# Mixing stage of a two-layer trunk: two weight casts a layer on GpSimd, two kinds of VectorE instruction pinned in program order, and the pooled products in another order

## The chip, the cores and the metric

The kernel runs on one core of one Trainium2 chip. The metric is the device time of one execution in microseconds. The kernel before has a median of 1299.72 us over three runs (1299.27 to 1299.83).

## The reference

A trunk of two layers works on 256 positions of 1024 channels in float32. Each layer is a feed-forward half step, a mixing stage with three branches, a second half step and an embedding added through a gate. Cut to what matters here:

```python
def layer(h):
    h = h + 0.5 * swiglu(rmsnorm(h, ffn1_norm), ffn1_w_gate, ffn1_w_up, ffn1_w_down)
    u = rmsnorm(h, mix_norm)
    (q, c_kv, q_idx, w_idx, k_idx, x_pool, z, xbc, dt_raw, gate_raw) = split(u @ w_in)
    y_attn = dsa_attention(q, rmsnorm(c_kv), q_idx, w_idx, rmsnorm(k_idx), w_uk, w_uv)
    y_pool = pool_mixer(x_pool, pool_w, pool_scale)      # windows 2, 4, 8, 16: mean less identity
    y_ssd = ssd_mixer(z, xbc, dt_raw, ...)               # Mamba-2, 2 chunks of 128
    g_attn, g_pool, g_ssd = split(sigmoid(gate_raw), 3)
    h = h + (g_attn * (y_attn @ w_br_attn) + g_pool * (y_pool @ w_br_pool)
             + g_ssd * (y_ssd @ w_br_ssd)) @ w_out
    h = h + 0.5 * swiglu(rmsnorm(h, ffn2_norm), ffn2_w_gate, ffn2_w_up, ffn2_w_down)
    return h + sigmoid(rmsnorm(h, ple_norm) @ ple_w_gate) * (p @ ple_w_proj)
# two layers, then a last rmsnorm
```

The attention chooses 64 keys for each position by an indexer's scores, and then takes a softmax over them with 8 heads. The Mamba branch multiplies by decay factors, which are exponentials of running sums of rates. The pooled branch is a running mean over a window, less the input, times a small matrix for each of four groups of 128 channels.

## The kernel before

Activations lie transposed, with channels on the partitions and the 256 positions along a row. To keep float32 accuracy on TensorE, every number is split in two parts in the format that PE multiplies here (fp32r in the rows): a high part (a cast) and a low part (the number less its high part). Each product is then three matmuls into one bank: high weight by high activation, high weight by low activation, low weight by high activation. In `mm3` these are lines 211, 212 and 213.

Weights come in units of 128 x 1024. `load` (lines 141 to 150) issues the load on the queue of SyncE (L144), the cast to the high part `whi` on ScalarE (L145) and the subtraction that gives the low part `wlo` on VectorE (L146). Four raw buffers and five each for the parts go round, and a unit is loaded up to four units ahead of its use. So a unit passes through a DMA, ScalarE and VectorE before PE can have all of it, and a cast can begin only when PE has done with the unit that had the buffer. One of the five pairs is kept for the matrix of the pooled branch during the mixing.

The mixing projects the input with 56 column tiles, one unit each. The last 24 (units `U_IN` + 32 to `U_IN` + 55) are the gates. While PE works through them, the Mamba states (`ssd`), the softmax (`softmax`, `attention`) and the pooled groups (`pool_group`) run on the other engines. They are four generators, and `weave` takes steps from them in turns by a number of steps that each is given. This stretch lies near 290 to 370 us in layer 0 and 643 us later in layer 1.

A scheduler that runs when the program is built puts the instructions of each engine in order, by durations and waits that it estimates for itself. It may move an instruction past others of its engine. Two marks hold it back: `keep_in_program_order`, which keeps the marked instructions of an engine in the order in which they are written, and the issue tokens of `turn`. Each engine then works through its list strictly in that order, and an instruction that waits holds up all behind it.

The lines that the change and the prediction speak of:

- In `softmax`, for each of two groups of scores: the maxima with the mask added (L921, VectorE, reading the scores in PSUM), the exponentials with their sums (L923, ScalarE), the reciprocal of the sums (L925, VectorE), the scaling (L927, ScalarE), and then PE's transposes (L114), copied out of PSUM in L939. The first softmax is over 128 keys, the later ones over 256.
- In `ssd`: the running sums of the rates (L1099, scans on VectorE), their exponentials (L1104, ScalarE), a copy of the last column (L1107), the product of the decay factors with a matrix `cb` (L1108, VectorE), the addition of a finished part (L1124), and a second kind of scan and exponential (L1135, L1136). GpSimd multiplies the input by the step size in L1085.
- In `pool_group`: the window sums by doubling, a copy and an add for each (L1168, L1169), a correction of the first columns (L1173), the mean less the input (L1176), its high part on ScalarE (L1181) and its low part (L1183), for one group on GpSimd and for the others on VectorE. The three products follow in L1188 by way of `mm3`.
- L256 and L260 are low parts of other activations (`split` and `split_scaled`), L259 is the high part that goes with L260.

## Time and profile before

| | |
|---|---|
| median of 3 runs | 1299.72 us |
| the profiled execution | 1300.84 us, span 1299.1 us |
| PE busy | 1290.3 us (99%), clock 1.000 |
| VectorE (DVE) busy | 1046.3 us (81%) |
| ScalarE (ACT) busy | 739.5 us (57%) |
| GpSimd (POOL) busy | 17.9 us (1%) in 27 instructions |
| casts of weight units (L145) | 456 of them, 1045 ns each |
| subtractions for the low part (L146) | 456 of them, 1215 ns each |
| the stretch 290 to 365 us (75 us) | PE 74.35, DVE 64.96, ACT 53.91, POOL 5.73 us busy |

In a row of the timeline the first number is the start in us from the span's beginning, the second the duration; then come engine, line, operation, output and inputs, shapes and count. A bracket gives the idle time of the engine just before and what ended it. An instruction's duration includes its end in the pipeline, so that the next one on the same engine can start some 0.1 us before it is over. PE and PEld are the matmuls and the weight loads that go with them. A matmul's duration (276 ns) is longer than the step from one to the next for the same reason.

### The profile page before, as it was taken

Reading aid. Unit: us, or ns where it says so; the run is one execution under the profiler, and the core shown is the slowest. Engines: PE = TensorE matmul, PEld = TensorE weight load, DVE = VectorE, ACT = ScalarE, POOL = GpSimd, SP = SyncE. Lnnn points to the kernel's source line nnn. Section 1 sums busy time; section 2 is a strip of 40 time slices with the busy share of each in tenths; the row PEclk is TensorE's granted clock in tenths of the full one; section 3 lists DMA queues with packets and bytes.
Section 4 is the critical chain, followed back from the end, with each engine's and each line's share of the span. In section 5 each row is a group of like instructions: output and inputs, shape, how many; then the busy total and the mean of one; then the engine's idle time right before and its main releaser. Section 6 shows DMA issues by size and latency. Waiting matters only on the chain.

```text
span 1299.1 us, 28286 instructions
## 1 busy us (share of the span) xinstructions
PE 1290.3 (99%) x11398; PEld 1282.0 (99%) x11398; DVE 1046.3 (81%) x1935; ACT 739.5 (57%) x1209; POOL 17.9 (1%) x27
## 2 busy tenths in 40 slices
PE   9999999999999999999999999999999999999998
PEld 9999999999999999999999999999999999999998
DVE  7877669987999887766997776799879989777667
ACT  6644446666874555544654444476667646544455
POOL 0000000000000000000000000000100000000000
PEclk9999999999999999999999999999999999999999
DMA  7766646586647576666556665556965566655661
GB/s 251 247 193 195 194 158 211 179 222 205 188 142 235 162 227 194 195 191 194 188 195 194 194 196 191 162 192 184 212 224 165 183 199 211 197 195 193 194 194 66
DMA packets 89571, 250.51 MB, mean 193 GB/s; under 512 B 25184, under 2 KB 27872, under 8 KB 89440
## 3 DMA queue, kind: packets, MB, share of 16 engines
q1 hardware_dynamic: 89008, 247.92, 60.6%
q8 instruction: 89, 1.46, 0.5%
q10 hardware_dynamic: 432, 0.79, 0.2%
q14 instruction: 42, 0.34, 0.1%
HBM read 245.50 MB, written 1.08 MB: 190 GB/s over the span
## 4 chain that ended last, share of the span: by engine, by line
PE 87%; DVE 7%; ACT 2%; DMA 2%; issue 2%; DVEq 0%; SPq 0%; ACTq 0%
PE mm L213 27%; PE mm L212 27%; PE mm L211 27%; DVE wlo L146 2%; DVE ct L1099 1%; PE aux L111 1%; ACT whi L145 1%; DMA gh<-rates 1%; DMA raw<-in_w_dram 1%; PE mm L230 1%; PE mm L227 1%; PE aux L213 1%; PE aux L212 1%; ACT t L923 1%; PE mm L225 1%
## 5 line engine op out<-in xcount | busy, mean ns | idle before, releaser
L145 ACT CAST whi<-raw 128x1024 fp32r<-128x1024 f32 (+1 forms) x456 | 475.1, 1045 | 484.9 <-PE mm L212 353.8
L146 DVE TENSOR_TENSOR wlo<-raw,whi 128x1024 fp32r<-128x1024 f32 (+1 forms) x456 | 552.2, 1215 | 170.1 <-ACT whi L145 162.2
L212 PE MATMUL mm<-ul,whi 128*128 128x256 f32 x2438 | 672.0, 276 | 0.0
L213 PE MATMUL mm<-uh,wlo 128*128 128x256 f32 x2438 | 671.8, 277 | 0.0
L211 PE MATMUL mm<-uh,whi 128*128 128x256 f32 x2402 | 662.3, 277 | 0.8 <-ACT whi L145 0.8
L212 PEld LDWEIGHTS mm<-ul,whi 128*128 128x128 f32 x2438 | 457.5, 188 | 0.1
L213 PEld LDWEIGHTS mm<-uh,wlo 128*128 128x128 f32 x2438 | 457.0, 188 | 0.2
L211 PEld LDWEIGHTS mm<-uh,whi 128*128 128x128 f32 x2402 | 449.8, 188 | 2.1 <-ACT whi L145 1.2
L213 PE MATMUL mm<-gh,wlo 128*128 128x256 f32 x704 | 194.1, 276 | 0.0
L212 PE MATMUL mm<-gl,whi 128*128 128x256 f32 x704 | 194.1, 276 | 0.0
L211 PE MATMUL mm<-gh,whi 128*128 128x256 f32 x704 | 193.7, 276 | 0.0
L213 PEld LDWEIGHTS mm<-gh,wlo 128*128 128x128 f32 x704 | 132.2, 188 | 0.0
L212 PEld LDWEIGHTS mm<-gl,whi 128*128 128x128 f32 x704 | 132.2, 188 | 0.0
L211 PEld LDWEIGHTS mm<-gh,whi 128*128 128x128 f32 x704 | 131.9, 188 | 0.0
L212 PE MATMUL mm<-a,whi 128*128 128x256 f32 x256 | 70.7, 276 | 0.0
L213 PE MATMUL mm<-a,wlo 128*128 128x256 f32 x256 | 70.7, 276 | 0.0
L211 PE MATMUL mm<-a,whi 128*128 128x256 f32 x256 | 70.7, 276 | 0.0
L213 PEld LDWEIGHTS mm<-a,wlo 128*128 128x128 f32 x256 | 48.1, 188 | 0.0
L211 PEld LDWEIGHTS mm<-a,whi 128*128 128x128 f32 x256 | 48.1, 188 | 0.0
L212 PEld LDWEIGHTS mm<-a,whi 128*128 128x128 f32 x256 | 48.1, 188 | 0.0
L498 DVE TENSOR_TENSOR t<-mm,rs_r 128x256 f32<-128x256 f32 x88 | 37.3, 424 | 13.2 <-PE mm L213 13.0
L499 DVE TENSOR_TENSOR t<-t,mm 128x256 f32<-128x256 f32 x87 | 36.5, 420 | 2.6
(300 smaller groups left out, 1271.1 us busy)
## 6 DMA issues: line engine op xcount, KB each, us to landing
raw<-in_w_dram SPq DMA_DIRECT2D x446, 512.0 KB, 4.3
gh<-rates SPq DMA_DIRECT2D x16, 256.0 KB, 4.1
raw<-in_w_dram SPq DMA_DIRECT2D x8, 352.0 KB, 3.0
ul<-a SPq DMA_DIRECT2D x32, 64.0 KB, 4.8
a<-in_x_dram SPq DMA_DIRECT2D x3, 512.0 KB, 5.3
gh<-rates SPq DMA_DIRECT2D x8, 128.0 KB, 4.5
a<-in_x_dram SPq DMA_DIRECT2D x1, 544.0 KB, 3.7
raw<-in_w_dram SPq DMA_DIRECT2D x2, 256.0 KB, 4.4
```

Of the source, the lines that this page charges most:

```text
L111: self.tc.keep_in_program_order(self.nc.tensor.matmul(*args, **kw))
L145: nc.scalar.copy(hi[:, :n], raw[:, :n])
L146: ins = nc.vector.tensor_tensor(lo[:, :n], raw[:, :n], hi[:, :n].bitcast(F), op=OP.subtract)
L211: (self.mm if keep else mm)(ps, a[0], b[0], start=start, stop=False)
L212: mm(ps, a[0], b[1], start=False, stop=False)
L213: mm(ps, a[1], b[0], start=False, stop=stop)
L225: (self.mm if keep and k == 0 else mm)(ps, w[0][:, s], u[0][:, k], start=k == 0, stop=False)
L227: mm(ps, w[0][:, s], u[1][:, k], start=False, stop=False)
L230: mm(ps, w[1][:, k * P:(k + 1) * P], u[0][:, k], start=False, stop=k == last)
L498: ins = [nc.vector.tensor_tensor(t, p1[0], r, op=OP.mult), nc.vector.tensor_tensor(g, t, p1[1], op=OP.mult)]
L499: nc.vector.tensor_tensor(g, t, p1[1], op=OP.mult)]
L923: self.last = nc.scalar.activation(pr[:, j], pr[:, j], AF.Exp, bias=x, scale=-1.0, accum_out=sums[:, j:j + 1])
```

## The change

Four edits, all in the mixing:

1. In `load`, two units of each layer, `U_IN` + 45 and `U_IN` + 54 (gate tiles 13 and 22), have their high part cast by GpSimd instead of ScalarE. In the lists below these are `whi_4329` and `whi_4869` in layer 0.
2. The reciprocal in `softmax` is kept in program order.
3. The decay product in `ssd` is kept in program order.
4. In `pool_group` the three matmuls are written out, so that the low weight by the high activation comes second and the high weight by the low activation last.

```diff
--- before.py
+++ after.py
@@ -142,7 +142,10 @@
         nc = self.nc
         raw, hi, lo = self.parts()
         nc.sync.dma_start(raw[:, :n], self.ins["w"][layer, u, :, :n])
-        nc.scalar.copy(hi[:, :n], raw[:, :n])
+        if u in (U_IN + 45, U_IN + 54):
+            nc.gpsimd.tensor_copy(hi[:, :n], raw[:, :n])
+        else:
+            nc.scalar.copy(hi[:, :n], raw[:, :n])
         ins = nc.vector.tensor_tensor(lo[:, :n], raw[:, :n], hi[:, :n].bitcast(F), op=OP.subtract)
         if keep:
             self.tc.keep_in_program_order(ins)
@@ -922,7 +925,7 @@
                                                1.0, 3.0e38, OP.add, OP.min, accum_out=x)
                 self.last = nc.scalar.activation(pr[:, j], pr[:, j], AF.Exp, bias=x, scale=-1.0,
                                                  accum_out=sums[:, j:j + 1])
-            nc.vector.reciprocal(sums, sums)
+            self.tc.keep_in_program_order(nc.vector.reciprocal(sums, sums))
             for j in range(per):
                 nc.scalar.mul(pr[:, j], pr[:, j], sums[:, j:j + 1])
             prs.append(pr)
@@ -1105,8 +1108,8 @@
                     if h == 0:
                         k = g * 8 + q * 4
                         nc.vector.tensor_copy(e0[:, k:k + 4], m[:, :, P - 1])
-                    nc.vector.tensor_tensor(m, m, cb[:, h, g, None].to_broadcast([P, 4, P]),
-                                            op=OP.mult)
+                    self.tc.keep_in_program_order(nc.vector.tensor_tensor(
+                        m, m, cb[:, h, g, None].to_broadcast([P, 4, P]), op=OP.mult))
                     yield
                 ps = self.bank("aux")
 
@@ -1185,7 +1188,8 @@
         yield
         po = self.bank()
         s = slice(g * P, (g + 1) * P)
-        self.mm3(po[:, :S], (wpl[0][:, s], wpl[1][:, s]), (yh, yl), True, True)
+        for w, v in ((0, yh), (1, yh), (0, yl)):
+            nc.tensor.matmul(po[:, :S], wpl[w][:, s], v, start=w == 0 and v is yh, stop=v is yl)
         self.split_scaled(yp[:, 0, g], yp[:, 1, g], po[:, :S], self.col(layer, "pool_scale", g))
```

From `load` on, a line of the kernel after has a number that is 3 higher than before, and 4 higher behind `pool_group`.

The edits move other instructions too, since the scheduler works out a new order. The queue of loads keeps its order, but for a load of the rates and a unit that change places once in each layer. GpSimd's list gets one cast behind the four products of L1085 and one behind the low part of the pooled group (L1183). On PE the transposes of the first softmax come eight matmuls earlier, ahead of the first use of `whi_4329`. The three places that follow are in layer 0; layer 1 has the same ones.

VectorE, from the unit `wlo_4747` to the first maxima of the last softmax (`t_692`); `t_700` and `t_701` are window sums, `t_681` is the mean less the input of the group whose low part GpSimd makes, `ct_4853` are the decay factors, and `uh_2747` is the Mamba branch's result. Before:

```order
L146 TENSOR_TENSOR wlo_4747<-raw_4745,whi_4746 128x1024
L1176 SCALAR_TENSOR_TENSOR t_681_4783<-t_675_4741,gl_2475 128x256
L146 TENSOR_TENSOR wlo_4792<-raw_4790,whi_4791 128x1024
L1124 TENSOR_TENSOR uh_2747<-uh_2747,aux_4789 128x4x128
L1099 SCALAR_TENSOR_TENSOR ct_4853<-gh_2474,after 128x512 x2
L1168 COPY t_700_4892<-gl_2475 128x1
L1169 TENSOR_TENSOR t_700_4892<-gl_2475 128x271
L921 ISA t_692_4857,mx_4858<-aux_4837,idxw_3617 128x256
```

and now:

```order
L1179 SCALAR_TENSOR_TENSOR t_681_4783<-t_675_4741,gl_2475 128x256
L149 TENSOR_TENSOR wlo_4747<-raw_4745,whi_4746 128x1024
L1171 COPY t_700_4892<-gl_2475 128x1
L1172 TENSOR_TENSOR t_700_4892<-gl_2475 128x271
L1127 TENSOR_TENSOR uh_2747<-uh_2747,aux_4789 128x4x128
L1102 SCALAR_TENSOR_TENSOR ct_4853<-gh_2474,after 128x512 x2
L149 TENSOR_TENSOR wlo_4792<-raw_4790,whi_4791 128x1024
L1171 COPY t_701_4895<-t_700_4892 128x2
L1172 TENSOR_TENSOR t_701_4895<-t_700_4892 128x270
L924 ISA t_692_4857,mx_4858<-aux_4837,idxw_3617 128x256
```

The mean `t_681` went ahead of the unit `wlo_4747`, the unit `wlo_4792` behind the scans, the window sum `t_700` ahead of the addition, and the copy and the add of the next window sum, `t_701`, came ahead of the maxima.

The same engine behind those maxima, down to the second reciprocal of the softmax (`sum_4859` and `sum_4908` belong to its two groups; `a_542_3897` holds the low parts of the attention's and the pooled branch's results). Before:

```order
L1108 TENSOR_TENSOR ct_4853<-ct_4853,gl_2475 128x512
L1168 COPY t_701_4895<-t_700_4892 128x2
L1169 TENSOR_TENSOR t_701_4895<-t_700_4892 128x270
L1108 TENSOR_TENSOR ct_4853<-ct_4853,gl_2475 128x512
L260 SCALAR_TENSOR_TENSOR a_542_3897<-mm_4886,cc_88,a_542_3897 128x256
L925 RECIPROCAL sum_4859<-sum_4859 128x2
L1168 COPY t_702_4898<-t_701_4895 128x4
L1169 TENSOR_TENSOR t_702_4898<-t_701_4895 128x268
L925 RECIPROCAL sum_4908<-sum_4908 128x2
```

and now:

```order
L1111 TENSOR_TENSOR ct_4853<-ct_4853,gl_2475 128x512
L1171 COPY t_702_4898<-t_701_4895 128x4
L1172 TENSOR_TENSOR t_702_4898<-t_701_4895 128x268
L263 SCALAR_TENSOR_TENSOR a_542_3897<-mm_4886,cc_88,a_542_3897 128x256
L928 RECIPROCAL sum_4859<-sum_4859 128x2
L1171 COPY t_703_4901<-t_702_4898 128x8
L1172 TENSOR_TENSOR t_703_4901<-t_702_4898 128x264
L1111 TENSOR_TENSOR ct_4853<-ct_4853,gl_2475 128x512
L928 RECIPROCAL sum_4908<-sum_4908 128x2
```

The second decay product stood ahead of both reciprocals and is now between them; the window sum `t_702` went ahead of the first reciprocal and `t_703` ahead of the second. PE meanwhile has the transposes of this softmax four matmuls earlier: twelve matmuls of the unit `whi_4746` are left behind the first of them, where eight were.

ScalarE, some 25 us earlier, from the copies of the first softmax's transposes (`aux_4412`, `aux_4413`) to the exponential of the decay factors; `t_646` is the exponential of the second kind (L1136), which waits for VectorE's scans of L1135. Before:

```order
L939 COPY t_627_4422<-aux_4412 128x512
L259 ACTIVATE a_542_3897<-mm_4458,cc_88 128x256
L939 COPY t_628_4425<-aux_4413 128x512
L145 CAST whi_4466<-raw_4465 128x1024
L1136 ACTIVATE t_646_4560<-t_646_4560 128x512
L145 CAST whi_4484<-raw_4483 128x1024
L690 ACTIVATE gh_2474<-mm_4427 128x512
L255 CAST a_542_3897<-aux_4533 128x4x128
L1104 ACTIVATE ct_4717<-ct_4717 128x512 x2
```

and now:

```order
L942 COPY t_627_4422<-aux_4412 128x512
L262 ACTIVATE a_542_3897<-mm_4458,cc_88 128x256
L942 COPY t_628_4425<-aux_4413 128x512
L1139 ACTIVATE t_646_4560<-t_646_4560 128x512
L148 CAST whi_4466<-raw_4465 128x1024
L148 CAST whi_4484<-raw_4483 128x1024
L693 ACTIVATE gh_2474<-mm_4427 128x512
L258 CAST a_542_3897<-aux_4533 128x4x128
L1107 ACTIVATE ct_4717<-ct_4717 128x512 x2
```

The cast of the unit `whi_4466` stood ahead of the exponential of `t_646` and now stands behind it.

## The prediction

> **What bounds the kernel now.** I read the page first, then the waits of PE, then the windows around the two places that the change touches, and last the instructions in order of time there.

> ```profile
> span 1299.1 us, 28286 instructions
> PE 1290.3 (99%) x11398; PEld 1282.0 (99%) x11398; DVE 1046.3 (81%) x1935; ACT 739.5 (57%) x1209; POOL 17.9 (1%) x27
> PE aux L114 <- ACT t L927: 0.8, 2, 0.4
> 333.10:361.10 28.00, 28.00 (x275) 27.06 (x272) 27.97 (x66) 21.95 (x50) 1.22 (x1) 1.00 0.58 178
> ```

> PE is busy for 99% of the span, and its granted clock is 1.00, so the end is set by PE's list of matmuls plus the few places where PE has to wait. Off PE nothing counts until it makes PE wait. The row of waits (us in total, times, longest) belongs to the softmax of layer 0 and its twin in layer 1. The last row is the window 333.1 to 361.1 of layer 0's mixing (columns: length, then PE, PEld, DVE, ACT, POOL, clock, DMA): VectorE is busy for 27.97 of 28.00 us there. It has no slack in that window, so whatever makes it late at the start is still late at the end.

> There are three stalls per layer that the change can touch. In layer 0:

> ```profile
> 323.92 1.03 ACT L145 CAST whi<-raw 128x1024 fp32r<-128x1024 f32 x1
> 324.35 0.28 PE L212 MATMUL mm<-ul,whi 128*128 128x256 f32 x1
> 324.46 0.28 PE L213 MATMUL mm<-uh,wlo 128*128 128x256 f32 x1
> 325.00 0.39 PE L211 MATMUL mm<-uh,whi 128*128 128x256 f32 x1 [0.27 <-ACT whi L145]
> 325.65 0.30 PE L114 MATMUL aux<-ident,t 128*128 128x128 f32 x1
> 355.14 0.19 PEld L212 LDWEIGHTS mm<-t,whi 128*128 128x128 f32 x1 [0.20 <-POOL t L1183]
> 358.11 0.51 ACT L923 ACTIVATE t<-t,mx 128x256 f32<-128x256 f32 x1
> 360.45 1.05 ACT L145 CAST whi<-raw 128x1024 fp32r<-128x1024 f32 x1
> 361.39 1.71 ACT L927 ACTIVATE t<-t,sum 128x256 f32<-128x256 f32 x4
> 361.95 0.44 PE L114 MATMUL aux<-ident,t 128*128 128x128 f32 x2 [0.38 <-ACT t L927]
> 967.28 0.28 PE L213 MATMUL mm<-uh,wlo 128*128 128x256 f32 x1
> 967.51 0.39 PE L211 MATMUL mm<-uh,whi 128*128 128x256 f32 x1
> ```

> Matmuls follow each other every 0.11 us (324.35, 324.46). **Stall A**, at 325.00: due at 324.57, so 0.43 is lost; the cast of 323.92 ends last. In layer 1 the same spot loses 0.12 (967.28 to 967.51, less 0.11). **Stall C**, at 355.14: the weight load waits 0.20 for GpSimd's low part of the pooled average; a restart costs 0.11 more (the matmul of 325.00 shows 0.39 instead of 0.28), together 0.3. **Stall B**, at 361.95: the transposes wait for the scaling L927, which stands behind the cast of 360.45. I count 0.55 lost, so PE asked at 361.40 (the bracket, 0.38, leaves out the load ahead of it). A, B and C of both layers together are 0.43 + 0.12 + 2 x (0.55 + 0.3) = 2.2 us, a few restarts more at most. That is all that the change can win: 0.17% of the time.

> **The change part by part.** *Two casts per layer leave ScalarE.* Each frees 0.94 us of its queue (360.45 to 361.39), just ahead of the scaling that PE waits for. That is the gain of B, if the scaling can use it.

> *VectorE's order around stall B.* These rows are the old order:

> ```profile
> 353.27 1.22 DVE L146 TENSOR_TENSOR wlo<-raw,whi 128x1024 fp32r<-128x1024 f32 x1
> 355.00 2.34 DVE L1099 TENSOR_TENSOR_SCAN ct<-gh,after 128x512 f32<-128x512 f32 x2
> 357.30 0.43 DVE L1169 TENSOR_TENSOR t<-gl 128x271 f32<-128x271 f32 x1
> 357.64 0.42 DVE L921 CUSTOM_DVE_ANT_0 t<-aux,idxw 128x256 f32<-128x256 f32 x1
> 359.02 0.69 DVE L1108 TENSOR_TENSOR ct<-ct,gl 128x512 f32<-128x512 f32 x1
> 359.62 0.16 DVE L1168 COPY t<-t 128x2 f32<-128x2 f32 x1
> 360.04 0.69 DVE L1108 TENSOR_TENSOR ct<-ct,gl 128x512 f32<-128x512 f32 x1
> 360.64 0.48 DVE L260 SCALAR_TENSOR_TENSOR a<-mm,cc,a 128x256 fp32r<-128x256 f32 x1
> 361.04 0.16 DVE L925 RECIPROCAL sum<-sum 128x2 f32<-128x2 f32 x1
> ```

> In the new order most of this is only permuted ahead of the four maxima (L921): split, scans and first doubling are still all in front. New in front is the second doubling, copy and add: 359.62 to 360.04, **0.42 us**. Behind the maxima come one decay product (359.02 to 359.62, 0.60), the third doubling (0.42), L260 (0.40) and only then the first reciprocal: maxima end + 1.42. The maxima take 357.64 to 359.02, 1.38.

> *A delay that arrives from upstream.* ScalarE's new order puts the cast of one unit behind the decay exponential L1136:

> ```profile
> 332.86 0.63 ACT L1136 ACTIVATE t<-t 128x512 f32<-128x512 f32 x1 [0.60 <-DVE t L1135]
> 333.12 1.22 DVE L146 TENSOR_TENSOR wlo<-raw,whi 128x1024 fp32r<-128x1024 f32 x1
> ```

> The cast used to be done before the exponential. Behind it (its 0.53 from 332.86) the cast starts at 333.39 and its split 0.94 later, at 334.33 instead of 333.12: 1.21 late. If the 0.94 that ScalarE saves at stall A brings all this forward, 0.27 late. I take **0.4**, near the lower end, since the queue between is ScalarE's own; VectorE's full window carries it to B.

> *The casts on GpSimd.* Its price is not in this trace. Rows to bound it (the first gives the shortest, median and longest of eight in ns):

> ```profile
> L1085 POOL TENSOR_TENSOR ul<-ul,dt x8: 1036/1038/1905, 289.6 to 936.6; 128x512 f32<-128x512 f32 x8
> L409 POOL TENSOR_SCALAR_AFFINE_SELECT tri<-ones 128x128 f32<-128x128 f32 x1 | 0.3, 290 | 0.0
> L405 POOL MEMSET ones<- 128x128 f32 x1 | 0.2, 204 | 0.3 <-POOLq L1476 0.3
> L1258 POOL TENSOR_SCALAR idxw<-idxw 128x256 f32<-128x256 f32 x1 | 0.9, 856 | 27.7 <-DMA idxw<-in_gn_dram 27.7
> L176 POOL MEMSET warm<- 128x1 f32 x1 | 0.1, 98 | 0.0
> ```

> By the memset (106 ns for 127 more elements) 1024 elements take 0.95 us; by the select 1.6; by the product with two inputs (1038 for 512) 2.1; by the scaling L1258 3.4. The cast has one input and no arithmetic and is nearest to the memset and the select: I take 1.1 us, ends 0.95 and 3.4. Even at 2.1 the casts are done long before PE needs them.

> *What they do to VectorE.* The trace holds a warning:

> ```profile
> 289.27 0.19 DVE L1030 SCALAR_TENSOR_TENSOR dt<-dt_y,dt_x 128x32 f32<-128x32 f32 x1
> 289.38 1.23 DVE L146 TENSOR_TENSOR wlo<-raw,whi 128x1024 fp32r<-128x1024 f32 x1
> 289.60 4.91 POOL L1085 TENSOR_TENSOR ul<-ul,dt 128x512 f32<-128x512 f32 x4 [22.69 <-DMA raw<-in_w_dram]
> 290.52 1.03 DVE L1031 SCALAR_TENSOR_TENSOR da<-dt,al 128x32 f32<-128x32 f32 x1
> 353.87 1.22 POOL L1183 TENSOR_TENSOR t<-t,t 128x256 fp32r<-128x256 f32 x1 [59.36 <-ACT t L1181]
> ```

> The first of the four GpSimd products, started under a split, takes 1.905 where the median is 1.038. And L1031, of the size of L1030's 0.19, takes 1.03 and ends with that product (291.5). GpSimd waited for the split; then VectorE's next instruction waited for GpSimd. L1183 at 353.87 also ends 0.6 after the split of 353.27 to 354.49. So an instruction of VectorE that reads two operands from SBUF and one of GpSimd exclude one another, whole instruction by whole instruction, and the one that has waited goes first. [...]

> At stall B two GpSimd instructions now meet VectorE in its full window. The subtraction L1183 moves up, because L1176 does, to the end of the previous split; the first doubling add, two SBUF operands, waits behind it: **0.4** (0.6 less the copy and what was overlapped). And the second cast, second in GpSimd's queue, waits for PE to free its buffer:

> ```profile
> 319.13 0.28 PE L111 MATMUL mm<-uh,whi 128*128 128x256 f32 x1
> 319.22 0.29 DVE L921 CUSTOM_DVE_ANT_0 t<-aux,idxw 128x128 f32<-128x128 f32 x1
> 356.87 0.28 PE L111 MATMUL mm<-uh,whi 128*128 128x256 f32 x1
> ```

> At 356.87 PE goes on to its next unit, which frees the buffer; after the change that is at 356.6 to 356.9. VectorE is then at the end of the scans, and next is a split of 1.2 us, then the maxima. The cast gets in, and the split waits for it: **1.0** (1.1 less the overlap at its start). At A the first cast's buffer comes free at 319.13, and it falls on the eight maxima, one of them at 319.22, which read their scores from PSUM; it is hidden there unless it lasts over 1.2 us or so, and what follows then is a decay product from SBUF.

> *Sum at B.* Maxima at 357.64 + 0.42 + 0.4 + 0.4 + 1.0 = 359.86. First exponential 0.47 behind (358.11 less 357.64), the last done 2.34 later (358.11 to 360.45): 362.67. First reciprocal at 359.86 + 1.38 + 1.42 = 362.66. So scaling from 362.7, transposes 0.56 behind (361.39 to 361.95), at 363.3. PE asks for them at 361.40, less 0.45, since its new order has them four matmuls earlier, less 0.3 for C: 360.65. Stall 2.6 instead of 0.55. The second reciprocal stands behind the second decay product, 1.1 behind the first; the transposes that need it are asked for 1.2 behind the first ones, so it adds nothing.

> *Stall C* goes: the low part is now read last and made earlier, minus 0.3. *Stall A*: scaling 0.93 earlier (323.92 to 324.85 was the cast), transposes at 324.7 instead of 325.65; PE asks for them eight matmuls (0.90) and the old stall (0.43) earlier, at 324.3; so 0.4 is lost again, and 0 to 0.4 in layer 1: nothing gained. The three pooled products and the reciprocals have the same counts and durations as before; the one queue of loads keeps its order but for one swap.

> Per layer 2.6 - 0.55 - 0.3 = +1.75, together **+3.5 us**. Against the profiled execution (1300.84, span 1299.1) that is 1304.3; the median shown is 1.1 lower, so 1299.7 + 3.5 = **1303.2 us**.

> **The rivals.** *No exclusion that matters* (the cast slips in beside the scans, or waits until VectorE reads PSUM): the 0.4 and the 1.0 go, maxima at 358.46, transposes at 361.9, stall 1.2, +0.35 a layer: 1300.4. For it: the scan is not among the rows that show the exclusion, and one shift of 1 us puts the cast on the maxima. Against: VectorE's next instruction is a split whichever way. *Relief* (the other side): ScalarE's free 0.94 decides and the stalls vanish, -2.2 to -2.6: 1297.3. It needs the scaling to start by 360.1 (360.65 less 0.56), so the maxima no later than 357.3, 0.3 earlier than now, while the new order alone puts them 0.42 later. Nothing but a shorter upstream speaks for it. *A long cast*, from 1.9 us up: at 2.1 the hold at B is 2.0, +1.0 a layer, and at A the decay products (two SBUF operands) wait too, 0.4 a layer: +6.3, 1306.0; at 3.4, B +2.3 and A about +1 a layer: +10, 1310. For it L1258's 856 ns for 256 elements; against, the select and the memset.

> **How the numbers follow.** 0.2%, 2.6 us, is about what a measurement of this kernel can tell. Forecast (1301.5 to 1305.5) 0.50, of which 0.06 is under 1302.3; no exclusion 0.25, all within; long cast 0.17, all slower; relief 0.08, half of it under 1297.1. Faster 0.04, same 0.06 + 0.25 + 0.04 = 0.35, slower 0.44 + 0.17 = 0.61. The range, 1298.8 to 1306.5, leaves out most of relief and about half of the long casts.

> **What would show it.** GpSimd: four casts of 0.95 to 1.6 us, more where VectorE held them up. VectorE: in each layer one split near 356.6 (999 in layer 1) of 2 us instead of 1.22, and a doubling add of 0.8 instead of 0.43. PE: no wait for GpSimd's low part, and two waits for the scaling of over 2 us each. I am wrong if those waits are under 1 us, if the splits beside the casts keep 1.22, or if the cast takes over 2 us.

## The result: 1308.09 us, 0.58% slower

The kernel after takes 1308.09 us, the median of six executions (1306.16 to 1308.81). The kernel before, run beside it, takes 1299.93 us (1299.27 to 1301.05, also six). The ratio is 1.0058, 95% interval 1.0047 to 1.0069. The forecast was 1303.2 us with a range up to 1306.5, so the sign was right and the size was more than twice what was forecast: 8.2 us instead of 3.5.

The profiled execution after took 1308.4 us with a span of 1306.2. Before, these were 1300.84 and 1299.1, so 7.1 us of the 7.6 between the two profiled executions lie inside the span. These are the lines of the page and of PE's waits that answer to those shown before:

```profile
span 1306.2 us, 28282 instructions
PE 1293.3 (99%) x11398; PEld 1285.6 (98%) x11398; DVE 1050.1 (80%) x1935; ACT 735.8 (56%) x1205; POOL 23.8 (2%) x31
```

```profile
PE aux L114 <- ACT t L930: 5.6, 3, 2.6
PE mm L214 <- ACT whi L148: 0.2, 1, 0.2
```

Two things stand there. PE's waits for the scaling went from 0.8 to 5.6 us, with a longest of 2.6, and the wait for GpSimd's low part (stall C) is gone. PE's *busy* time also went up by 3.0 us with the same 11398 matmuls, which no wait explains.

**The steps up to stall B, read in the timeline.** VectorE and GpSimd in layer 0 (start in us, duration, engine, line, operation, tiles, shapes, count, idle time before):

```profile
353.08 1.22 DVE L149 TENSOR_TENSOR wlo<-raw,whi 128x1024 fp32r<-128x1024 f32 x1
354.28 0.92 DVE L1172 TENSOR_TENSOR t<-gl 128x271 f32<-128x271 f32 x1
355.72 2.33 DVE L1102 TENSOR_TENSOR_SCAN ct<-gh,after 128x512 f32<-128x512 f32 x2
357.97 2.00 DVE L149 TENSOR_TENSOR wlo<-raw,whi 128x1024 fp32r<-128x1024 f32 x1
359.95 0.43 DVE L1172 TENSOR_TENSOR t<-t 128x270 f32<-128x270 f32 x1
360.31 0.41 DVE L924 CUSTOM_DVE_ANT_0 t<-aux,idxw 128x256 f32<-128x256 f32 x1
363.10 0.15 DVE L928 RECIPROCAL sum<-sum 128x2 f32<-128x2 f32 x1
```

```profile
319.70 1.04 POOL L146 CAST whi<-raw 128x1024 fp32r<-128x1024 f32 x1 [24.74 <-DVE mx L924]
353.68 1.22 POOL L1186 TENSOR_TENSOR t<-t,t 128x256 fp32r<-128x256 f32 x1 [32.94 <-ACT t L1184]
357.07 1.81 POOL L146 CAST whi<-raw 128x1024 fp32r<-128x1024 f32 x1 [2.17 <-PE mm L215]
```

GpSimd's subtraction L1186 was ready at 353.68, waited for the split of 353.08 and ended at 354.90; the doubling add behind it took 0.92 instead of 0.43. The second cast became ready at 357.07 under the scans and lasted 1.81, where the undisturbed one at 319.70 takes 1.04. I read the difference, 0.77, as its wait for the scan; then the split waited for the cast: 2.00 instead of 1.22. So the maxima start at 360.31 instead of 357.64 and the first reciprocal runs at 363.10. Layer 1 has the same picture: the add 0.92 at 999.91, the cast 1.74 at 1002.76, the split 1.99 at 1003.59.

**The stall and what follows it.** PE after, and its granted clock in windows across the stall (columns as before: stretch, length, PE, PEld, DVE, ACT, POOL, clock, DMA share, GB/s):

```profile
360.92 0.28 PE L216 MATMUL mm<-uh,wlo 128*128 128x256 f32 x1
363.84 0.44 PE L114 MATMUL aux<-ident,t 128*128 128x128 f32 x2 [2.65 <-ACT t L930]
...
366.05 0.41 PE L215 MATMUL mm<-ul,whi 128*128 128x256 f32 x1
...
368.23 0.28 PE L215 MATMUL mm<-ul,whi 128*128 128x256 f32 x1
...
370.95 0.77 PE L111 MATMUL aux<-ct,ul 128*64 128x128 f32 x10
```

```profile
361.00:363.80 2.80, 0.20 (x2) 0.00 (x0) 2.80 (x14) 2.72 (x11) 0.00 (x0) 1.00 0.50 183
363.80:365.00 1.20, 1.16 (x9) 1.16 (x10) 1.17 (x5) 1.03 (x3) 0.00 (x0) 0.83 0.05 14
365.00:366.00 1.00, 1.00 (x6) 1.00 (x6) 0.99 (x1) 1.00 (x2) 0.00 (x0) 0.50 0.00 0
...
367.00:368.00 1.00, 1.00 (x7) 1.00 (x7) 1.00 (x3) 1.00 (x3) 0.00 (x0) 0.50 0.76 229
368.00:369.00 1.00, 1.00 (x10) 1.00 (x10) 1.00 (x4) 0.91 (x1) 0.00 (x0) 1.00 0.82 303
```

The transposes were due 0.11 behind the matmul of 360.92 and came at 363.84: 2.81 lost where it was 0.55. **Then PE worked at half clock.** The clock is 1.00 until the transposes are under way, 0.50 in the windows from 365 to 368 (the one left out too), and 1.00 again. A window of 1.20 us with a mean of 0.83 holds 0.41 us at half, so the drop begins at 364.6; it ends at 368.0 and lasts 3.4 us. In it a matmul of 256 columns takes 0.41 us instead of 0.28, and one follows the other in 0.21 instead of 0.11. That is where the extra busy time of PE comes from. In layer 1 it is the same thing again:

```profile
1006.55 0.28 PE L216 MATMUL mm<-uh,wlo 128*128 128x256 f32 x1
1009.47 0.49 PE L114 MATMUL aux<-ident,t 128*128 128x128 f32 x2 [2.64 <-ACT t L930]
```

```profile
1009.40:1011.00 1.60, 1.53 (x8) 1.54 (x9) 1.56 (x5) 1.43 (x5) 0.00 (x0) 0.60 0.02 5
...
1012.00:1013.00 1.00, 1.00 (x7) 1.00 (x7) 1.00 (x1) 1.00 (x4) 0.00 (x0) 0.50 0.45 86
```

**The account.** To measure the price of one place I take the same matmul in both kernels ahead of it and behind it. Two pairs of layer 0, with these rows of the kernel before:

```profile
360.84 0.28 PE L213 MATMUL mm<-uh,wlo 128*128 128x256 f32 x1
...
366.98 0.88 PE L111 MATMUL aux<-ct,ul 128*64 128x128 f32 x12
```

The matmul ahead of the stall is 0.08 late (360.92 against 360.84), the first of the decay group behind the slow stretch 3.97 (370.95 against 366.98). So stall B with what follows costs 3.89 us in layer 0, and by the same pairing 3.84 in layer 1. Of the 3.89 the stall itself is 2.81 - 0.55 = 2.26; the remaining 1.63 are the half clock (the same 50 matmuls lie between the two of a pair, and half of 3.4 us is 1.7). Both layers together make 7.7, against 7.1 in the span: the first loads add 0.44; stall C gives back 0.28 and 0.29 as forecast, stall A 0.07 and 0.28, and a wait near 850 us 0.3; 0.1 more is spread over the rest.

### The profile page after: what moved, and what is told of

It reads as the page before. It is cut to its first block, busy times and chain, and to the rows that moved or that the text cites. A ratio compares the mean times of both kernels' runs of the same rounds, so it can differ in the third digit from the quotient of the medians.

```text
span 1306.2 us, 28282 instructions
## 1 busy us (share of the span) xinstructions
PE 1293.3 (99%) x11398; PEld 1285.6 (98%) x11398; DVE 1050.1 (80%) x1935; ACT 735.8 (56%) x1205; POOL 23.8 (2%) x31
## 4 chain that ended last, share of the span: by engine, by line
PE 91%; DVE 5%; DMA 1%; ACT 1%; issue 1%; SPq 0%; DVEq 0%; POOL 0%; ACTq 0%; POOLq 0%
PE mm L216 28%; PE mm L215 28%; PE mm L214 28%; PE aux L111 1%; DVE wlo L149 1%; DVE ct L1102 1%; DMA raw<-in_w_dram 1%; PE aux L215 1%; PE aux L216 1%; PE aux L214 1%; PE mm L230 1%; PE mm L233 1%; PE aux L114 1%; PE mm L228 1%; ACT whi L148 1%
```

## Experiments

The first theory was that of the prediction: the casts on GpSimd exclude VectorE's instructions in its full window, and the lateness goes to PE at stall B. Its rival was that the new order alone does it. When the result came out at twice the size, a second part was added: PE's long standing still makes its clock fall for a stretch, and that costs as much again; the rival is that further waits cost it. Ratios are to the kernel before on the same chip, with 95% intervals.

**1. The casts alone.** Edit 1 without the other three:

```diff
-        nc.scalar.copy(hi[:, :n], raw[:, :n])
+        if u in (U_IN + 45, U_IN + 54):
+            nc.gpsimd.tensor_copy(hi[:, :n], raw[:, :n])
+        else:
+            nc.scalar.copy(hi[:, :n], raw[:, :n])
```

> The two casts per layer on GpSimd, and none of the other three edits. Theory (the casts make VectorE wait, the softmax comes late, PE stalls, and the stall halves PE's clock for a while): the casts alone carry the whole loss. With the old order of the pooled products PE waits some 0.4 us for the low part just ahead, so the one long stall per layer should be about 2.4 us instead of 2.8. If a stall of 2.4 us still trips the clock, 1307 to 1308 us; if not, 3.3 us less, about 1304. Rival (the pinned instructions and the new order make the stall): close to 1300.

Measured: 1308.79 us, ratio 1.0066 (1.0051 to 1.0081). The casts alone carry the whole loss, a little above the 1307 to 1308 expected. The stalls are 2.67 and 2.69 instead of the 2.4 expected. The parts are not quite those of the change: in the profiled execution the clock fell in layer 0 only, and PE waits 1.10 us at 325 and 0.94 at 852, where the change has hardly a wait. The split behind the scans is held up as in the change:

```profile
359.15 1.99 DVE L149 TENSOR_TENSOR wlo<-raw,whi 128x1024 fp32r<-128x1024 f32 x1
```

**2. The other three edits, no casts on GpSimd.** `load` as before:

```diff
-            nc.vector.reciprocal(sums, sums)
+            self.tc.keep_in_program_order(nc.vector.reciprocal(sums, sums))
-                    nc.vector.tensor_tensor(m, m, cb[...], op=OP.mult)
+                    self.tc.keep_in_program_order(nc.vector.tensor_tensor(m, m, cb[...], op=OP.mult))
-        self.mm3(po[:, :S], (wpl[0][:, s], wpl[1][:, s]), (yh, yl), True, True)
+        for w, v in ((0, yh), (1, yh), (0, yl)):
+            nc.tensor.matmul(po[:, :S], wpl[w][:, s], v, start=w == 0 and v is yh, stop=v is yl)
```

> The reciprocals and decay products pinned and the pooled products in the new order, with all casts on ScalarE as before. Theory: nothing is lost without the casts, 1299.4 to 1300.4 us; the wait for GpSimd's low part goes, and the transposes take over most of what it gave (stall 0.55 to about 0.8). Rival (pins and order make the stall): 1303 or more, with stalls of 2 us at the transposes.

Measured: 1301.22 us over ten executions, ratio 1.0006 (0.9996 to 1.0015), no difference that can be told. The maxima and the second doubling keep the order of the kernel before, the add takes its 0.43, and the stall is nearly as before (0.52 in the bracket against 0.38):

```profile
363.33 0.44 PE L114 MATMUL aux<-ident,t 128*128 128x128 f32 x2 [0.52 <-ACT t L927]
```

So neither the two marks nor the order of the pooled products makes a difference that shows in the time, and the new order on VectorE, too, comes with the casts: the scheduler works out another order once a cast has left ScalarE.

**3. The change without its edit 4** (the pooled products in their old order):

```diff
-        for w, v in ((0, yh), (1, yh), (0, yl)):
-            nc.tensor.matmul(po[:, :S], wpl[w][:, s], v, start=w == 0 and v is yh, stop=v is yl)
+        self.mm3(po[:, :S], (wpl[0][:, s], wpl[1][:, s]), (yh, yl), True, True)
```

> The change without its fourth edit: the pooled products go back to the old order. The delays of the other engines are the same; PE waits some 0.4 us for the low part first and then 2.4 us instead of 2.8 for the transposes. If the loss is delay alone, the same time as the change, 1308. If the clock falls only after a stall that is long enough, and 2.4 us is not, 1304.5 to 1305; the clock column behind the stall decides. Rival for the clock (it falls because of what GpSimd does, not because PE stands still): low clock as in the change.

Measured: 1306.48 us (1304.55 to 1307.81), ratio 1.0047 (1.0032 to 1.0062). The stall is hardly shorter than in the change, against the expectation. But this run gave the best evidence on the clock, by chance. In its profiled execution, the fastest of the four (1304.55), both stalls are there and the clock stays at 1.00 behind them:

```profile
362.89 0.44 PE L114 MATMUL aux<-ident,t 128*128 128x128 f32 x2 [2.64 <-ACT t L930]
```

```profile
360.20:362.90 2.70, 0.06 (x2) 0.01 (x1) 2.70 (x12) 2.61 (x11) 0.00 (x0) 1.00 0.59 188
362.90:365.00 2.10, 2.10 (x18) 2.10 (x19) 2.07 (x5) 1.93 (x4) 0.00 (x0) 1.00 0.04 8
```

Its span is 1302.8, that is 3.4 us below that of the change, with the same stalls. Two drops of 1.6 us are 3.2. The other three fit: 1305.47 with a mean clock of 0.999, and 1307.81 and 1307.49 with 0.998 and 0.997. So the same wait can cost 1.6 us more or not, and its length alone doesn't decide.

**4. Four more matmuls ahead of the transposes.** They fill part of the stall with 512-column products into the bank that the transposes overwrite (the change, and in `softmax`, for the last softmax of a layer):

```diff
+        self.smx = getattr(self, "smx", 0) + 1
+        for _ in range(4 if self.smx % 3 == 0 else 0):
+            self.mm(pts[0], self.onesr, self.onesr[:, None, :].to_broadcast([P, 4, P]),
+                    start=True, stop=True)
```

> The change, with four matmuls of 512 columns ahead of the transposes of each layer's last softmax; their result is overwritten by the transposes. They need nothing that is late, so PE has 0.85 us of work inside the stall, which shrinks to about 1.9 us in layer 0 and 2.5 in layer 1. Theory: the late softmax is as late as before, so without the clock nothing is won, and with a full clock 3.3 us are: 1305. If the clock falls after 2.5 us but not after 1.9, 1306.5. Rival (GpSimd's work or the lateness itself lowers the clock): 1308, with a clock of 0.5 behind both.

Measured: 1307.24 us (1306.55 to 1307.47), ratio 1.0053 (1.0038 to 1.0068). The waits are 1.73 and 1.57 instead of 2.65 and 2.64, and still the clock fell in layer 0, though not in layer 1:

```profile
363.56 0.98 PE L114 MATMUL aux<-ident,t 128*128 128x128 f32 x4 [1.73 <-ACT t L930]
```

```profile
364.10:367.50 3.40, 3.40 (x17) 3.40 (x17) 3.12 (x6) 3.40 (x7) 0.00 (x0) 0.50 0.22 46
```

A stall of 1.73 dropped the clock here and one of 2.64 did not in experiment 3. The time is a miss: the other three executions have a mean clock of 0.999, where the one drop of the profiled execution gave 0.998, and they took 1306.55 to 1307.40, hardly less than the one with a drop (1307.47) and well above the 1305 expected. What else the four matmuls cost was not traced, so this run doesn't price the clock either.

**5 and 6. One cast at a time:** gate tile 22 alone, then gate tile 13 alone, on the kernel before:

```diff
-        nc.scalar.copy(hi[:, :n], raw[:, :n])
+        if u in (U_IN + 54,):        # experiment 6: U_IN + 45
+            nc.gpsimd.tensor_copy(hi[:, :n], raw[:, :n])
+        else:
+            nc.scalar.copy(hi[:, :n], raw[:, :n])
```

> Only the second cast (gate tile 22) on GpSimd, nothing else changed. ScalarE is relieved of it right ahead of the scaling that PE waits for, and nothing else is much reordered. Theory (GpSimd's read of SBUF shuts out VectorE's split): the split beside it takes about 2 us instead of 1.22, the stall at the transposes is 1.1 to 1.5 us in each layer instead of 0.55, +1 to +2 us, 1301 to 1302; a stall that short leaves the clock at 1.0. Rival (order and lateness alone, no exclusion): no change or a few tenths faster, 1299.5 to 1300.

Measured with tile 22: 1302.38 us over ten executions, ratio 1.0009 (1.0000 to 1.0018). The order is nearly that of before, so it is the doubling add, not the split, that follows the scans, and it is held up instead:

```profile
357.21 1.20 POOL L146 CAST whi<-raw 128x1024 fp32r<-128x1024 f32 x1 [1.89 <-PE mm L215]
```

```profile
357.53 1.17 DVE L1172 TENSOR_TENSOR t<-gl 128x271 f32<-128x271 f32 x1
```

1.17 instead of 0.43 is 0.74 late, and the stall is 1.09 where the kernel before has 0.38 in the bracket: 0.71 more. What the cast takes from VectorE arrives at PE in full. The clock stays at 1.00 (a matmul of 256 columns behind the stall takes 0.28 us, where at half clock it takes 0.41).

> Only the first cast (gate tile 13) on GpSimd, nothing else changed. This cast falls on VectorE's maxima from PSUM, so it should hold nothing up, but with it comes the new order in which a unit's cast stands behind the decay exponential. Theory: +1 to +2.3 us from that lateness and from the subtraction on GpSimd that holds up one add, stalls of 0.9 to 1.3 us at the transposes of the last softmax, clock 1.0, 1301 to 1302. Rival (each cast costs its own hold): no stall beyond 0.6 at the transposes, under 1300.5.

Measured with tile 13: 1303.33 us over ten executions, ratio 1.0023 (1.0014 to 1.0032). The stall is 1.82, more than I expected. Its cast holds nothing up (1.04 us, on the maxima), and the split of 357.64 keeps 1.19; but the order is the new one, with the add held by the subtraction (0.91), the second doubling and a decay product (0.61) ahead of the maxima, and on ScalarE a cast of a unit between two exponentials. So the order that comes with this cast is a loss by itself. In layer 1 of the profiled execution the clock fell behind the stall of 1.82 us, in layer 0 it did not behind an equal one:

```profile
363.80:366.20 2.40, 2.40 (x21) 2.40 (x22) 2.26 (x6) 2.40 (x6) 0.00 (x0) 1.00 0.50 121
```

```profile
1008.00:1011.40 3.40, 3.40 (x18) 3.40 (x17) 2.49 (x3) 3.01 (x6) 0.00 (x0) 0.50 0.76 228
```

The ten executions of this one kernel divide by it. Seven have a mean clock of 0.999 or more and took 1302.43 to 1303.48 us; the three with 0.998 or 0.997 took 1304.40, 1305.91 and 1306.59.

**7. GpSimd only writes.** The cast is replaced by a memset of the same tile, so that GpSimd writes as much and reads nothing from SBUF (the units' high part is then 1.0, the cast is left out). The question is whether VectorE is held up by GpSimd's reading:

```diff
-            nc.gpsimd.tensor_copy(hi[:, :n], raw[:, :n])
+            nc.gpsimd.memset(hi[:, :n].bitcast(F), 1.0)
```

> The change, but GpSimd fills the high part of the two units with the constant 1.0 instead of casting the raw weights: it leaves out the cast, and VectorE's low part is the raw value less 1. So GpSimd writes the same 128 x 1024 to SBUF and reads nothing. [...] Rival (any GpSimd access excludes): the split takes 1.7 to 2.2 us, as beside the cast.

Measured in one execution: 1303.6 us. The memset lasts 0.96 us and the doubling add runs under it in its own time:

```profile
358.27 0.96 POOL L146 MEMSET whi<- 128x1024 f32 x1 [1.76 <-PE mm L215]
```

```profile
358.73 0.44 DVE L1172 TENSOR_TENSOR t<-gl 128x271 f32<-128x271 f32 x1
```

0.44 beside a memset, 1.17 behind a cast that started 0.32 ahead of it (experiment 5): in this pair it was GpSimd's reading that excluded VectorE, not its writing and not its being busy. The order in this kernel is another one, so its time isn't compared.

**8 and 9. Other units.** Gate tiles 6 and 12 instead, whose casts fall at 295 and 313 us, ahead of the full window; first edit 1 alone, then all four edits:

```diff
-        if u in (U_IN + 45, U_IN + 54):
+        if u in (U_IN + 38, U_IN + 44):
```

> Two other units per layer are cast by GpSimd, gate tiles 6 and 12 (U_IN + 38 and U_IN + 44), and the other three edits are left out. By the trace these casts fall on stretches in which GpSimd is free and VectorE reads PSUM or waits, near 294 and 312 us. Theory (a cast costs only where it shuts VectorE out in its full window, and ScalarE's relief is a gain elsewhere): the stalls at 325 and 362 us shrink, about -1.8 us, 1298 to 1299. Rival (any cast on GpSimd costs VectorE about 1 us on the path): +1 to +2 us.

> The change word for word, with all four edits, but the two units that GpSimd casts are gate tiles 6 and 12 (U_IN + 38 and U_IN + 44) instead of 13 and 22. Theory (which cast goes to GpSimd decides alone; the other three edits cost nothing): about 2 us faster than the kernel before, 1298 to 1299, no stall over 1 us at the transposes, clock 1.0. Rival (the pins or the order of the products are part of the loss): slower than before, 1301 or more.

Measured over eleven executions each: 1298.34 us, ratio 0.9988 (0.9979 to 0.9996), and 1299.11 us, ratio 0.9989 (0.9980 to 0.9998). These rows are from the first. The casts take 1.06 us on average, and the transposes wait no longer than before:

```profile
L146 POOL CAST whi<-raw 128x1024 fp32r<-128x1024 f32 x4 | 4.3, 1064 | 31.9 <-DVE gl L750 16.3 <-PE mm L215 15.6
```

```profile
362.06 0.44 PE L114 MATMUL aux<-ident,t 128*128 128x128 f32 x2 [0.38 <-ACT t L930]
```

The second cast of layer 0 (at 312.56) held an instruction of VectorE up here too:

```profile
312.58 1.30 DVE L1179 SCALAR_TENSOR_TENSOR t<-t,gl 128x256 f32<-128x256 f32 x1
```

It takes 0.42 undisturbed, so 0.9 was lost; but PE waits for nothing between 310 and 345 us there. So the idea of the change isn't wrong; where the two units stand decides, by whether VectorE's lateness reaches PE. The first of the two has the lowest median of this study; by their ratios the two can't be told apart. The gain, 0.12%, is below the 0.2% that the prediction gives as the limit of a measurement; only the many executions (eleven, against 27 of the kernel before) keep the interval just below 1. The profiled execution was one of its slower ones (1300.57 us): against the kernel before, PE is 0.7 us late there after the first loads and 0.4 more after 848 us. By pairs of matmuls it gains 0.6 and 0.3 at stall A, and in layer 1 0.3 at C and 0.6 at B.

**10. The cast of tile 22 twice.** The change, and a second identical cast behind it, so that the stall passes one period of the clock:

```diff
             nc.gpsimd.tensor_copy(hi[:, :n], raw[:, :n])
+            if u == U_IN + 54:
+                nc.gpsimd.tensor_copy(hi[:, :n], raw[:, :n])
```

> The change, with the second unit (gate tile 22) cast twice by GpSimd, one cast behind the other with the same result. Theory: the split beside them is held longer, by up to another 1.0 us, and the stall at the transposes grows from 2.7 to 3.4 to 4.2 us. Of a stall that long at least 1.7 us fall into one of the clock's periods of 3.413 us wherever it lies, so the clock should fall in both layers in nearly every execution: 1309 to 1311. Rival (VectorE gets in between the two casts): as the change, 1307 to 1308.

Measured: 1312.2 us (1310.55 to 1313.31), ratio 1.0087 (1.0074 to 1.0101), a little above the range that I had given. The stalls are 3.51 and 3.48, 0.85 more than in the change, and behind them the clock is at half for two periods in both layers:

```profile
363.90:365.10 1.20, 0.05 (x1) 0.06 (x1) 1.20 (x6) 1.11 (x5) 0.00 (x0) 0.50 0.00 0
365.10:370.70 5.60, 5.60 (x27) 5.60 (x28) 3.40 (x11) 5.17 (x10) 0.00 (x0) 0.50 0.02 3
370.70:372.00 1.30, 1.30 (x13) 1.30 (x13) 1.30 (x2) 0.55 (x2) 0.00 (x0) 1.00 0.00 0
```

From 363.9 to 370.7 are 6.8 us, twice 3.4. PE stood still for the first 1.2 of them, so the slow work is 5.6 us long and loses 2.8, against 1.6 in the change. That and the longer stall, 0.85 + 1.2 in each layer, make 4.1 us; the medians differ by 4.1, the distances to the kernel before by 3.4.

**11. Eight more matmuls** instead of four:

```diff
-        for _ in range(4 if self.smx % 3 == 0 else 0):
+        for _ in range(8 if self.smx % 3 == 0 else 0):
```

> The change, with eight matmuls of 512 columns, 1.7 us, ahead of the transposes of each layer's last softmax; their result is overwritten by the transposes. Theory: PE then stands still for 1.0 to 1.6 us, less than what brought the clock down in the profiles so far (1.73 us in one period of 3.413 us), so the clock stays at 1.0 in both layers. The added matmuls delay what follows by 1 to 1.5 us, and 3.3 us are won: 1305.5 to 1306.5 against 1308. Rival (the clock falls because of the lateness or of GpSimd): 0.5 behind the stalls, 1309 to 1310.

Measured: 1308.78 us (1307.72 to 1309.76), ratio 1.0062 (1.0048 to 1.0076). On the clock the expectation held: it is 1.00 through both layers' mixing. The time is a miss all the same.

```profile
360.62 1.99 PE L111 MATMUL aux<-onesr 128*128 128x512 f32 x8
363.45 0.84 PE L114 MATMUL aux<-ident,t 128*128 128x128 f32 x4 [0.84 <-ACT t L930]
364.53 0.84 PE L114 MATMUL aux<-ident,t 128*128 128x128 f32 x4 [0.24 <-ACT t L930]
```

```profile
363.50:369.00 5.50, 4.92 (x36) 4.08 (x37) 5.22 (x12) 4.93 (x9) 0.00 (x0) 1.00 0.41 107
```

The transposes now stand in groups of four behind one another, so that the second group waits for its own scaling and the units between them no longer cover it: PE is busy for 4.92 of the 5.50 us after 363.5. In layer 1 there are waits of 0.8 and 0.9 at 954 and 971 us that the change doesn't have. What the clock saved was lost again, at least in part in these waits. So the run shows that a broken-up stall, here with no wait for the scaling over 0.9 us, left the clock alone, and doesn't price the clock.

**What the runs say of the clock together.** The rows show drops of 3.4 us, or twice that. The trace's record of the clock dates every change of it: 364.60 to 368.01 and 1009.71 to 1013.13 in the change, 363.87 to 370.70 in experiment 10. Within an execution all lie on one grid of 3.413 us: 1009.71 - 364.60 = 645.1, which is 189 times 3.413. So I counted, for each stall, how long PE stood still (from the end of the last matmul to the next start) in each period of this grid:

| run, layer | stands still, us | in one period and the next | clock behind it |
|---|---|---|---|
| change, 0 | 2.65 | 2.65 + 0 | half, one period |
| change, 1 | 2.64 | 2.64 + 0 | half, one period |
| 1, casts alone, 0 | 2.67 | 2.25 + 0.42 | half, one period |
| 1, casts alone, 1 | 2.69 | 1.20 + 1.49 | 1.00 |
| 3, 0 | 2.64 | 1.23 + 1.41 | 1.00 |
| 3, 1 | 2.50 | 1.77 + 0.73 | 1.00 |
| 4, 0 | 1.73 | 1.73 + 0 | half, one period |
| 4, 1 | 1.57 | 1.37 + 0.20 | 1.00 |
| 6, 0 | 1.82 | 0.96 + 0.86 | 1.00 |
| 6, 1 | 1.82 | 1.82 + 0 | half, one period |
| 10, 0 | 3.51 | 2.33 + 1.17 | half, two periods |
| 10, 1 | 3.48 | 2.49 + 0.99 | half, two periods |

Every drop begins at the end of a period in which PE stood still for 1.73 us or more, and no period with less begins one. There is one exception the other way, 1.77 in experiment 3 without a drop; the ends of matmuls are modelled in the trace, so 1.73 and 1.77 may not really differ. Once the clock is at half, less seems to do: in experiment 10, 1.17 and 0.99 us of standing still in the slow period kept it there for another. So about half a period of standing still was enough for a whole one at half clock. Against the work the grid lies differently in the profiled executions: the drop begins 0.76 us behind the start of the transposes in the change (364.60 and 363.84), and in experiment 10 1.18 ahead of it (363.87 and 365.05). Whether it also differs between the executions of one kernel was not traced; that would fit the scatter: of the six executions of the change, the five with a mean clock of 0.996 or 0.997 took 1306.78 to 1308.81, and the one with 0.999 was the fastest, 1306.16. (The clock also falls behind PE's last matmul, which ends 5.8 us before the end of the span: it is 0.50 from 1303.26 on, 275 of these periods behind 364.60, and that alone accounts for 0.999.) The fastest is 2.2 below the median of the five, where the pairs of rows give 3.2 for two drops; the six executions of the kernel before scatter by 1.8, so one execution doesn't settle the price. That half a period is the limit I have only read off these twelve stalls. No run set the phase at will; that the drop costs time with all else equal rests on the executions of one kernel with different mean clocks, in experiments 3 and 6.

## Why the prediction was right and wrong

- **What bounds the kernel, and where the change acts.** Right. Outside stalls A, B and C there is little: B costs 3.9 and 3.8 us, C gives 0.28 and 0.29 (forecast 0.3 each), A 0.07 and 0.28 (forecast nothing).
- **The cast's own price**, 1.1 taken, 0.95 to 3.4 as bounds: 1.04 undisturbed. The long cast, the rival with 0.17, is out: the time fell into its range for another reason.
- **The exclusion.** Right in kind, and near in size: the add was held 0.49 (forecast 0.4), the split 0.78 (forecast 1.0), at the places named, in both layers. But the split's hold came near in part by luck. The cast was ready at 357.07, well before the split's turn at 357.97, and would have been done at 358.11; it reached so far into the split only because the scan held it up. So the cast was held up behind scans with two operands from SBUF too (1.81 us instead of 1.04), which the rows of before did not show and the forecast did not count on. Under the memset, by which GpSimd only writes, the add kept 0.44 us. The rival without exclusion is refuted by the add of experiment 5 and the two holds in the change.
- **The second doubling, 0.42.** Right (359.95 to 360.31 and the copy ahead).
- **The delay from upstream, 0.4 between 0.27 and 1.21.** Too small. The split behind the decay exponential starts at 333.87 instead of 333.12, so 0.75 arrive. Holds of 1.27, the doubling's 0.42 and 0.75 make 2.44 of the 2.67 by which the maxima are late (forecast 2.22); 0.2 stay open.
- **Stall B, 2.6.** 2.81 and, in layer 1, also 2.81 (1006.55 to 1009.47, less 0.11). That it came so near is partly luck: the transposes came at 363.84 instead of 363.3, but PE asked for them at 361.03 instead of 360.65, because the first loads had made it 0.44 late, and most of the one error took away the other. Without the clock the change loses 7.1 - 1.63 - 1.58 = 3.9 us of span, where I had 3.5.
- **The sum at B, which failed.** It counted a stall of 2.6 us as 2.6 us: it let PE go on at the granted clock of 1.00 that the window of before shows. That window has no stall over 0.55, so it could not show what a longer one does. The clock at half for 3.41 us adds 1.63 in layer 0 and 1.58 in layer 1, 3.2 us in all. With it the sum would have been 1299.7 + 3.5 + 3.2 = 1306.4. Of the 1.7 us from there to 1308.1, 0.4 are the terms above, 0.5 the time outside the spans (2.2 against 1.74), 0.6 the profiled executions (before 0.9 above its median, after 0.3), and 0.2 the median of before, which is higher here.
- **Relief**, the rival on the other side: the scaling did come without the cast ahead of it, but the maxima were never early enough, as the prediction said. Experiment 9 shows the same edits with two other units at 0.9989.
- **What would show it.** Casts of 1.04 to 1.81, the add at 0.92, the split at 2.00 and 1.99, and waits of over 2 us came as described in size. The split came later than named (357.97 and 1003.59 instead of 356.6 and 999). The clock column was not on the list.

## What to carry to other kernels

Before moving work to GpSimd, look at what VectorE does at that moment: where its window was full and its instructions read two operands from SBUF, a cast of 1.04 us by GpSimd held VectorE up here by 0.74 and 0.78 us, and what VectorE lost in experiment 5 reached PE nearly in full (0.74 of lateness became 0.71 of stall). Other units, cast where VectorE has room, turned the loss of 0.6% into a gain of 0.1%. When a forecast makes PE wait for more than about half of 3.4 us (1.73 us was enough here), add the slow stretch behind it (here 1.6 us for each) as a term with a chance, and read the clock by windows just behind the stall, since the mean over the span (0.996) hides it. An edit that only changes which engine does a cast may also move the scheduler's whole order, so the order has to be compared, and the edit tried alone.

## What the runs showed of the hardware that I had not expected

```profile
359.31 1.92 POOL L148 CAST whi<-raw 128x1024 fp32r<-128x1024 f32 x1
```

```profile
360.25 1.00 DVE L1173 COPY t<-t 128x2 f32<-128x2 f32 x1
```

- A memset of 128x1024 by GpSimd (0.96 us) costs nearly as much of GpSimd as the cast (1.04), and the add of VectorE that ran under it kept its 0.44.
